# Layer 0's dense mixer takes 512 tokens of two streams in its first products

## The chip, the cores and the metric

The kernel runs on one core of a Trainium2 chip. The metric is the device time of one execution in microseconds (us). Three runs of the kernel before took 2129.68, 2131.46 and 2137.14 us; the median is 2131.46 us.

## The reference, cut to what matters

Two streams of 256 tokens by 1024 features go through two layers with the same weights: the context (CTX) and the latent stream (LAT). Only LAT is returned, so in layer 1 the context is needed for attention keys and values and for the RWKV states alone.

```python
for l in range(DEPTH):                      # DEPTH = 2
    o_lat, o_ctx = token_mixer(modulate(x, ...), modulate(xc, ...), ...)   # attention | RWKV-7 | Hyena
    x  = post_norm(alpha * x + g1 * o_lat, ...)
    xc = post_norm(alpha * xc + cg1 * o_ctx, ...)          # layer 0 only
    if l % 2 == 0:                                         # layer 0: the dense mixer
        f_lat, f_ctx = swiglu(modulate(x, ...), w1, w3, w2), swiglu(modulate(xc, ...), w1, w3, w2)
    else:                                                  # layer 1: experts, LAT only
        f_lat = moe_swiglu(...)
    xc = post_norm(alpha * xc + cg2 * f_ctx, ...)          # layer 0 only
    x  = post_norm(alpha * x + g2 * f_lat, ...)

def swiglu(h, w1, w3, w2):                  # 1024 -> 2816 -> 1024
    return (jax.nn.silu(h @ w1) * (h @ w3)) @ w2
```

In RWKV the latent scan of a layer starts from the final states of that layer's context scan.

## The kernel before, in words

Every weight is fp32 and is used as a pair: `wload` (L348 on) loads a 128x1024 chunk (`raw`, 512 KB by the queue of SP), and `split` (L315, L316) makes `whi` on ACT and the rest `wlo` on DVE. `mm3` (L321 to L323) multiplies two such pairs in three matmuls. Loads are chained in the order of the program (`behind`). The weight buffers have a kind per part of the program (`s.w`, with counts in `BUFS`: raw chunks and split pairs); "l" serves layer 0 and the beginning of layer 1, "n" the rest of layer 1 up to the experts.

The order on each engine is made by the framework's scheduler as the kernel is built: an instruction written earlier has precedence, and one written later may run ahead where the earlier ones wait. `order` adds an edge by hand that one instruction stands behind another. PSUM has eight banks under five tags (`BANKS`): g 3, a 2, w0, w1 and t one each.

The dense mixer (`ffn`) is done for one stream at a time. `hT` normalises and transposes 256 tokens into the pairs `hp`. `block` makes 256 of the 2816 inner features: four weight chunks of `fw13`, each with 8 weight tiles of 128x128 (`ab`, 24 matmuls with 256 columns of tokens), then tanh, gate and split into `ffg`. A stream has 11 blocks in two parts of 6 and 5. After each part `tok_mm` multiplies its `ffg` with `fw2` (`fo`, 512 columns, 12 matmuls a chunk), and `post_norm` gathers the parts (`pnr`), normalises and writes `x`. The last chunks of the last part go through `tok_last`, which finishes the first 128 tokens before the second.

The body (L1688 on) around it: layer 0's output projection for CTX, then Hyena for LAT; the context mixer's `hT`; the output projection for LAT (`wo`, L1290 on); the context mixer, with the modulation products of layer 1 (`ada`, 48 chunks in 3 rounds, fp32) as `fill`: one such chunk after each `wload`; the latent mixer up to its first block of part 2 (`s.some(f, 10)`). Then layer 1: `hT` and seven tiles of the input projection (`win`, `u`) for CTX, `rw_prep` and `rwkv` for CTX, the filter spectra of Hyena (`spectra`), and only then the rest of the latent mixer (`x = s.whole(f)`: four blocks and ten chunks of `fw2`). The latent half of layer 1 follows: `hT`, `win` for RWKV, `rw_prep`, `rwkv`, `win` for attention and the first two Hyena tiles, `attend` (8 rounds), the other Hyena tiles, `hyena`, `w_out`, `moe`.

RWKV has two directions; direction 0 uses bank w0 and direction 1 bank w1 for all its products. `rw_prep` begins with the product `rw` (L855, bank w0). The last step before the chain of states is the multiplication of `rN` (L1075); the chain itself is `rS` (L1089, L1091). `spectra` uses w0 (`hf1`, L542; up to `Kn`, read at L608), w1 and t (`hf_d`, L548).

```python
f = s.ffn(0, LAT, x[LAT])
s.some(f, 10)
s.ldlora(1)
gc = {"st": CTX, "h": s.hT(1, CTX, 0, xc)}
s.win(1, [0, 1, 2, 3, 4, 5, 6], gc)
s.rw_prep(1, gc)
S0 = s.rwkv(1, gc, None, None)
for _ in s.spectra(1, "w0", "t", "w1", *s.spec_load(1)()):
    pass
x = s.whole(f)
```

Of the kernel before, what the change touches and what calls it, by code (L numbers as in the profile page):

```python
# [143 lines left out]
def layout(i):  # L144
# [38 lines left out]
    A["fw13"] = w13(g("ffn_w1"), g("ffn_w3"))[0]  # L183
# [75 lines left out]
class Trunk:  # L259
# [183 lines left out]
    def hT(s, l, st, prm, src, f32=None):  # L443

        nc = s.nc
        dst = s.pairs("hp", "hp", "hp", "hp")
        xh = [s.k([128, 1024], "xhat") for _ in src]
        for i in range(2):
            s.ln_hat(src[i:i + 1], xh[i:i + 1])
        for kp in range(4):  # L450
            ps = s.bank("a", "hT").rearrange("p (k q) -> p k q", k=2)
            for k2 in range(2):
                k = 2 * kp + k2
                for i in range(2):
# [30 lines left out]
    def conv3(s, u, out, cp, cc, cn, bias):  # L485

        nc = s.nc
        if bias is None:
            nc.scalar.activation(out, u, AF.Copy, scale=cc)
        else:  # L490
            nc.scalar.activation(out, u, AF.Identity, scale=cc, bias=bias)
        nc.vector.scalar_tensor_tensor(out[:, 1:], u[:, :255], cp, out[:, 1:], op0=OP.mult, op1=OP.add)
        return nc.vector.scalar_tensor_tensor(out[:, :255], u[:, 1:], cn, out[:, :255], op0=OP.mult, op1=OP.add)


class Mix(Trunk):
# [117 lines left out]
    def hy_in(s, l, g, i, ps):  # L614
# [6 lines left out]
        s.conv3(ps, o, s.pv(l, "hw0", i), s.pv(l, "hw1", i), s.pv(l, "hw2", i), s.pv(l, "hb", i))  # L621
# [133 lines left out]
    def attend(s, l, g, oT):  # L755
# [9 lines left out]
        half, read = [slice(0, 64), slice(64, 128)], None  # L765
# [47 lines left out]
class Rwkv(Mix):  # L813
# [73 lines left out]
    def rw_dir(s, l, g, d, need_y):  # L887
# [258 lines left out]
    def rw_out(s, l, g, oT):  # L1146

        nc = s.nc
        vt, kf, kT = g["vt"], g["kf"], g["kT"]
        pr = s.k([128, 2, 256], "rro")  # L1150
        nc.vector.tensor_add(pr, kf[:, 0], kf[:, 1])
# [30 lines left out]
        nc.scalar.activation(sg[64:96], lo[64:96, :], AF.Tanh, scale=0.5)  # L1182
# [20 lines left out]
class Ffn(Rwkv):  # L1203
# [14 lines left out]
    def post_norm(s, l, st, which, x, parts, apart=()):  # L1218
# [18 lines left out]
        for n, o in enumerate(parts):  # L1237
            for h in range(2):
# [80 lines left out]
    def block(s, b, hp):  # L1319

        nc = s.nc
        ps = [s.bank("g", "ab") for _ in range(2)]
        for kh in range(4):
            hi, lo = s.wload(s.A["fw13"][b, kh])
            for n, p in enumerate(ps):
                for f in range(2):
                    for k in range(2):
                        ws = slice(512 * k + 256 * n + 128 * f, 512 * k + 256 * n + 128 * f + 128)

                        s.mm3(p[:, 256 * f:256 * f + 256], (hi[:, ws], lo[:, ws]), hp[2 * kh + k],  # L1330
                              kh == 0 and k == 0 and f == 0, kh == 3 and k == 1, skip_group_check=True)
# [4 lines left out]
        g = s.k([128, 2, 2, 256], "ffg", F32R)  # L1336
        s.split(t.rearrange("p (f t) -> p f t", f=2), g[:, 0], g[:, 1])
# [18 lines left out]
    def ffn(s, l, st, x):  # L1356

        hp = s.hT(l, st, 3, x)
        yield

        def part(b0, n):
            gt = []

            def o(h):
                for b in range(b0, b0 + n) if h == 0 else ():
                    gt.append(s.block(b, hp))
                    yield
                t2 = lambda i, k: tuple(gt[k // 2][m][:, k % 2, 128 * i:128 * i + 128] for m in range(2))
                banks = [s.bank("g", "fo") for _ in range(2)]
                src = lambda kh: s.A["fw2"][h, b0 + kh]  # L1370
                if h == 1 and b0 > 0:
                    s.tok_mm(src, t2, banks, 2 * n, range(n - 3))
                    s.tok_last([(src(kh), kh, banks) for kh in range(n - 3, n)], t2, 2 * n)
                else:
                    s.tok_mm(src, t2, banks, 2 * n)
# [5 lines left out]
        return (yield from s.post_norm(l, st, 1, x, [part(0, 6), part(6, 5)], (1,)))  # L1381
# [186 lines left out]
class Top(Ffn):  # L1568
# [4 lines left out]
    BUFS = {"a": (12, 0), "l": (6, 4), "n": (5, 4), "m": (30, 4)}  # L1573
# [84 lines left out]
    def body(s):  # L1658
# [64 lines left out]
        x = s.whole(f)  # L1723

        s.w = "n"
# [30 lines left out]
```

## Time and profile before

| what | value |
|---|---|
| median of 3 runs | 2131.46 us |
| the profiled execution's own time | 2134.47 us |
| its span, first to last instruction | 2132.7 us |
| TensorE (PE) busy | 2033.8 us, 95% |
| VectorE (DVE) busy | 1659.7 us, 78% |
| ScalarE (ACT) busy | 1105.6 us, 52% |
| mean granted TensorE clock | 0.965 of full speed |
| HBM read | 464.56 MB |

All times in the views count from the start of the span. Matmuls are pipelined: a matmul's duration overlaps the next one's, so the cost of one in a stream is the distance from start to start. A window's row gives the busy time of each engine with its count of instructions, the granted clock, and the share and rate of the DMA engines. The two layers share the span so: layer 0 up to about 868 us (its mixers up to 516, the dense mixer after that), layer 1 up to the experts from 868 to about 1260, the experts for the rest.

### The profile page before, as it was taken

To read this page: it belongs to the slowest core of one execution; us is meant where nothing else is said; L and a number is where in the kernel's file an instruction comes from. 1 tells how busy PE (TensorE), PEld (TensorE's weight loads), DVE (VectorE), ACT (ScalarE), POOL (GpSimd) and SP (SyncE) were. 2 spreads that over 40 slices of the span, in tenths; PEclk is the share of its full clock that TensorE was granted. 3 is DMA by queue.
4 is the path that set the end of the run, shared out by engine and by line. 5 is a ranking of instruction groups with operands and counts; after the bars stand their busy time and mean duration, and the time that the engine had idled before them with its cause. 6 is when DMAs were issued, how large, how long until landed. Compare 5 with 4: busy or idle time off the path is not lost. (4 is left out here: it accounts for less than half of the span.)

```text
span 2132.7 us, 35433 instructions
## 1 busy us (share of the span) xinstructions
PE 2033.8 (95%) x13514; PEld 1656.6 (78%) x13514; DVE 1659.7 (78%) x3050; ACT 1105.6 (52%) x1615; POOL 111.1 (5%) x87
## 2 busy tenths in 40 slices
PE   7999999999999999989798997999999999999996
PEld 2878777667878999888487676888888888888885
DVE  6897678469753685776888568799899989988997
ACT  3532445132332434443254232877787877778773
POOL 0012002100000000010101200000000000000000
PEclk9999899899999999999998997999999999999998
DMA  8522332246697545332311038699999999999992
GB/s 302 186 83 90 139 124 83 80 160 230 235 337 269 198 164 200 137 102 94 125 55 38 31 110 316 233 329 356 352 347 367 356 343 347 365 359 339 364 352 103
DMA packets 147850, 469.12 MB, mean 220 GB/s; under 512 B 31636, under 2 KB 33972, under 8 KB 147672
## 3 DMA queue, kind: packets, MB, share of 16 engines
q1 hardware_dynamic: 123512, 446.27, 57.9%
q0 software_dynamic: 4816, 17.36, 2.3%
q10 hardware_dynamic: 19344, 3.15, 0.8%
q8 instruction: 108, 1.77, 0.3%
q14 instruction: 70, 0.57, 0.1%
HBM read 464.56 MB, written 2.16 MB: 219 GB/s over the span
## 5 line engine op out<-in xcount | busy, mean ns | idle before, releaser
L316 DVE TENSOR_TENSOR wlo<-wraw,whi 128x1024 fp32r<-128x1024 f32 x748 | 887.4, 1221 | 83.0 <-ACT whi L315 52.4
L315 ACT CAST whi<-wraw 128x1024 fp32r<-128x1024 f32 x748 | 751.6, 1049 | 146.1 <-DMA wraw<-in_fw_dram 33.8
L321 PE MATMUL ab<-whi,m_x 128*128 128x512 f32 x704 | 281.6, 400 | 0.0
L323 PE MATMUL ab<-whi,m_x 128*128 128x512 f32 x704 | 275.6, 391 | 0.0
L322 PE MATMUL ab<-wlo,m_x 128*128 128x512 f32 x704 | 275.0, 391 | 0.0
L321 PE MATMUL ab<-hp,whi 128*128 128x256 f32 x704 | 204.9, 292 | 3.1 <-ACT hp L315 2.2
L323 PE MATMUL ab<-hp,wlo 128*128 128x256 f32 x704 | 201.8, 288 | 2.8 <-DVE wlo L316 2.8
L322 PE MATMUL ab<-hp,whi 128*128 128x256 f32 x704 | 201.4, 286 | 1.3 <-DVE hp L316 1.2
L321 PE MATMUL u<-hp,whi 128*128 128x256 f32 x512 | 152.0, 300 | 3.9 <-ACT hp L315 3.0
L323 PEld LDWEIGHTS ab<-whi,m_x 128*128 128x128 f32 x704 | 132.2, 188 | 28.3
L322 PEld LDWEIGHTS ab<-wlo,m_x 128*128 128x128 f32 x704 | 132.5, 188 | 25.5 <-DVE wlo L316 0.2
L321 PEld LDWEIGHTS ab<-whi,m_x 128*128 128x128 f32 x704 | 132.2, 188 | 25.1
L321 PEld LDWEIGHTS ab<-hp,whi 128*128 128x128 f32 x704 | 135.7, 193 | 19.0 <-issue 10.6
L323 PE MATMUL u<-hp,wlo 128*128 128x256 f32 x512 | 149.0, 294 | 1.4 <-DVE wlo L316 1.1
L322 PE MATMUL u<-hp,whi 128*128 128x256 f32 x512 | 149.5, 295 | 0.0
L323 PEld LDWEIGHTS ab<-hp,wlo 128*128 128x128 f32 x704 | 136.1, 194 | 6.3 <-DVE wlo L316 3.9
L322 PEld LDWEIGHTS ab<-hp,whi 128*128 128x128 f32 x704 | 136.4, 194 | 2.0 <-DVE hp L316 1.8
L321 PE MATMUL mo<-whi,ffg 128*128 128x512 f32 x352 | 137.8, 391 | 0.0
L323 PE MATMUL mo<-whi,ffg 128*128 128x512 f32 x352 | 137.1, 390 | 0.0
L322 PE MATMUL mo<-wlo,ffg 128*128 128x512 f32 x352 | 137.0, 389 | 0.0
L969 POOL TENSOR_TENSOR rBD<-rAT,cst 128x1024 f32<-128x1024 f32 x28 | 67.2, 2408 | 937.7 <-DVE rTm L959 506.9
L321 PEld LDWEIGHTS u<-hp,whi 128*128 128x128 f32 x512 | 99.6, 196 | 18.2 <-issue 9.6
(396 smaller groups left out, 3536.3 us busy)
## 6 DMA issues: line engine op xcount, KB each, us to landing
wraw<-in_mw_dram SPq DMA_DIRECT2D x495, 512.0 KB, 5.6
wraw<-in_fw_dram SPq DMA_DIRECT2D x132, 512.0 KB, 5.7
wraw<-in_adaw_dram SPq DMA_DIRECT2D x96, 512.0 KB, 4.4
wraw<-in_win_dram SPq DMA_DIRECT2D x64, 512.0 KB, 5.1
wraw<-in_mw_dram POOLq DMA_DIRECT2D x33, 512.0 KB, 6.7
wraw<-in_wout_dram SPq DMA_DIRECT2D x24, 512.0 KB, 4.2
lngb<-in_rows_dram SPq DMA_DIRECT2D x12, 512.0 KB, 7.3
x<-in_xs_dram SPq DMA_DIRECT2D x8, 512.0 KB, 5.6
```

Source lines behind the costliest of these rows:

```text
L315: i = (s.nc.scalar.copy if eng == "a" else s.nc.vector.tensor_copy)(hi, src)
L316: return i, s.nc.vector.tensor_sub(lo, src, hi.bitcast(F32))
L321: mm(out, a[0], b[0], start=start, stop=False, **kw)
L322: mm(out, a[0], b[1], start=False, stop=False, **kw)
L323: mm(out, a[1], b[0], start=False, stop=stop, **kw)
L969: i = nc.gpsimd.tensor_mul(x.rearrange("p u (j t) -> p u j t", j=4), bc(ATu[:, :, m, None, :], [128, 8, 4, 32]), bc(mask.rearrange("p (j t ...
```

## The change: what it does

- The dense mixer's blocks take both streams' 512 tokens at once. `fw13` is laid out anew on the host: 22 blocks of 128 features, two chunks each; a chunk's 24 matmuls have 512 columns. A block's two banks come in turn from g and a.
- The blocks go in three parts of 6, 8 and 8. After each of the first two parts the second products (`fw2`) are done for CTX and then LAT; after the third, CTX's are done in `ffn` and LAT's by `x = s.whole(f)`, now right behind layer 1's `hT` for CTX.
- Both streams' `hT` stand before the first block; 15 of the 48 `ada` chunks stand between CTX's and LAT's.
- Layer 1's context half therefore has none of the dense mixer behind it. `s.w = "n"` now holds from CTX's `win` on, with 4 raw chunks and 3 split pairs in place of 5 and 4.
- New edges: in `rw_out` (three uses) the first addition and the tanh of the gate stand behind the last multiplication of `rN` (`fed`); in layer 1's LAT the convolutions of the Hyena tiles and the first product of `attend` stand behind it too.

```diff
-    A["fw13"] = w13(g("ffn_w1"), g("ffn_w3"))[0]
+    u = w13(g("ffn_w1"), g("ffn_w3"))[0].reshape(11, 2, 2, 128, 2, 2, 2, 128)
+    A["fw13"] = np.ascontiguousarray(u.transpose(0, 6, 1, 3, 2, 4, 5, 7)).reshape(22, 2, 128, 4, 256)
...
-    def hT(s, l, st, prm, src, f32=None):
+    def hT(s, l, st, prm, src, dst=None):
-        dst = s.pairs("hp", "hp", "hp", "hp")
+        dst = dst or s.pairs("hp", "hp", "hp", "hp")
...
-    def conv3(s, u, out, cp, cc, cn, bias):
+    def conv3(s, u, out, cp, cc, cn, bias, after=None):
...
+        if after is not None:
+            s.order(i, after)
...
-    def attend(s, l, g, oT):
+    def attend(s, l, g, oT, read=None):
...
+        g["fed"] = fed
...
-        nc.vector.tensor_add(pr, kf[:, 0], kf[:, 1])
+        s.order(nc.vector.tensor_add(pr, kf[:, 0], kf[:, 1]), g["fed"])
...
-        nc.scalar.activation(sg[64:96], lo[64:96, :], AF.Tanh, scale=0.5)
+        s.order(nc.scalar.activation(sg[64:96], lo[64:96, :], AF.Tanh, scale=0.5), fed)
...
     def block(s, b, hp):
-        ps = [s.bank("g", "ab") for _ in range(2)]
-        for kh in range(4):
+        ps = [s.bank("ga"[b % 2], "ab") for _ in range(2)]
+        for kh in range(2):
             hi, lo = s.wload(s.A["fw13"][b, kh])
             for n, p in enumerate(ps):
-                for f in range(2):
-                    for k in range(2):
-                        ws = slice(512 * k + 256 * n + 128 * f, 512 * k + 256 * n + 128 * f + 128)
-                        s.mm3(p[:, 256 * f:256 * f + 256], (hi[:, ws], lo[:, ws]), hp[2 * kh + k],
-                              kh == 0 and k == 0 and f == 0, kh == 3 and k == 1, skip_group_check=True)
+                for k in range(4):
+                    ws = slice(256 * k + 128 * n, 256 * k + 128 * n + 128)
+                    s.mm3(p, (hi[:, ws], lo[:, ws]), hp[4 * kh + k], kh == 0 and k == 0, kh == 1 and k == 3)
...
+    PARTS = (0, 6), (6, 8), (14, 8)
...
+    def ffn(s, l, hp, x):
...
+        out = [s.post_norm(l, st, 1, x[st], [part(st, n) for n in range(3)], (1,), True) for st in range(2)]
+        for n, (b0, nb) in enumerate(s.PARTS):
+            gt[n] = []
+            for b in range(b0, b0 + nb):
+                gt[n].append(s.block(b, hp))
+            if n < 2:
+                for st in range(2):
+                    s.some(out[st], 4)
+        return s.whole(out[CTX]), out[LAT]
...
-    BUFS = {"a": (12, 0), "l": (6, 4), "n": (5, 4), "m": (30, 4)}
+    BUFS = {"a": (12, 0), "l": (6, 4), "n": (4, 3), "m": (30, 4)}
...
-        f = s.ffn(0, CTX, x[CTX])
-        s.some(f, 1)
+        hp, hs = s.ffn_in()
+        s.hT(0, CTX, 3, x[CTX], hs[CTX])
         x.append(s.w_out(0, 1, oT[1], None))
         s.fill = s.ada(1, [0, 1, 2])
-        xc = s.whole(f)
+        s.some(s.fill, 15)
+        s.hT(0, LAT, 3, x[LAT], hs[LAT])
+        xc, f = s.ffn(0, hp, x)
         s.drain()
-        f = s.ffn(0, LAT, x[LAT])
-        s.some(f, 10)
         s.ldlora(1)
         gc = {"st": CTX, "h": s.hT(1, CTX, 0, xc)}
+        x = s.whole(f)
+        s.w = "n"
         s.win(1, [0, 1, 2, 3, 4, 5, 6], gc)
         s.rw_prep(1, gc)
         S0 = s.rwkv(1, gc, None, None)
         for _ in s.spectra(1, "w0", "t", "w1", *s.spec_load(1)()):
             pass
-        x = s.whole(f)
-        s.w = "n"
...
+        gl["hyfed"] = gl["fed"]
         s.win(1, ATT + HY[:2], gl)
-        s.go(s.attend(1, gl, oT))
+        s.go(s.attend(1, gl, oT, gl["fed"]))
```

## Rows read from the trace of the kernel before

**Rows 1.** The page: engines' busy time, and the costliest group of instructions.
```profile
PE 2033.8 (95%) x13514; PEld 1656.6 (78%) x13514; DVE 1659.7 (78%) x3050; ACT 1105.6 (52%) x1615; POOL 111.1 (5%) x87
...
L316 DVE TENSOR_TENSOR wlo<-wraw,whi 128x1024 fp32r<-128x1024 f32 x748 | 887.4, 1221 | 83.0 <-ACT whi L315 52.4
```
**Rows 2.** Windows: stretch, length, busy PE, PEld, DVE, ACT, POOL, clock, DMA.
```profile
516.40:868.00 351.60, 346.73 (x2557) 299.93 (x2557) 219.29 (x354) 130.87 (x158) 0.00 (x0) 0.99 0.65 233
...
868.00:1200.00 332.00, 297.66 (x2605) 251.46 (x2605) 253.98 (x638) 138.69 (x252) 39.41 (x21) 0.95 0.25 80
```
**Rows 3.** Timeline of PE: start, duration, line; ten matmuls lie between the rows.
```profile
800.13 0.28 PE L321 MATMUL ab<-hp,whi 128*128 128x256 f32 x1
...
801.33 0.28 PE L322 MATMUL ab<-hp,whi 128*128 128x256 f32 x1
...
728.07 0.39 PE L322 MATMUL fo<-wlo,ffg 128*128 128x512 f32 x1
...
730.34 0.39 PE L323 MATMUL fo<-whi,ffg 128*128 128x512 f32 x1
```
**Rows 4.** Timeline of PE: one chunk of `ab` between two chunks of `ada`.
```profile
560.86 0.38 PE L321 MATMUL ab<-hp,whi 128*128 128x256 f32 x1
...
563.92 0.64 PE L392 MATMUL ada<-wraw,keep 128*32 128x256 f32 x8
564.49 0.38 PE L321 MATMUL ab<-hp,whi 128*128 128x256 f32 x1
```
**Rows 5.** Start: last `wo` (PE), LAT's second `xhat` (DVE); a window of `wlo` alone.
```profile
516.16 0.40 PE L323 MATMUL wo<-whi,oTh 128*128 128x512 f32 x1
...
555.34 0.81 DVE L441 TENSOR_SCALAR xhat<-x,keep 128x1024 f32<-128x1024 f32 x1
...
516.40:555.40 39.00, 21.27 (x77) 14.52 (x77) 13.32 (x11) 1.00 0.79 266
```
**Rows 6.** Timeline of PE: from CTX's last `fo` to LAT's `ab` at full rate.
```profile
745.98 0.39 PE L323 MATMUL fo<-whi,ffg 128*128 128x512 f32 x1
...
757.82 0.36 PE L321 MATMUL ab<-hp,whi 128*128 128x256 f32 x1
```
**Rows 7.** Timeline of PE: from LAT's last `fo` to layer 1's first `u` of LAT.
```profile
1053.80 0.39 PE L323 MATMUL fo<-whi,ffg 128*128 128x512 f32 x1
...
1066.60 0.69 PE L455 MATMUL hT<-keep,xhat 128*128 128x128 f32 x2 [12.41 <-DVE xhat L441]
...
1070.71 0.58 PE L321 MATMUL u<-hp,whi 128*128 128x256 f32 x1 [0.49 <-ACT hp L315]
```
**Rows 8.** Layer 1: CTX's first `u` and `rS`, LAT's `rw` and last `rN` (durations min/median/max).
```profile
870.55 0.48 PE L321 MATMUL u<-hp,whi 128*128 128x256 f32 x2
...
L1089 PE MATMUL rS<-rS,rMx x56: 218/275/323, 984.3 to 1005.0; 128*128 128x64 f32 x56
...
L855 PE MATMUL rw<-lora,rkl x4: 589/641/693, 1093.9 to 1096.7; 33*128 33x512 f32 x4
...
L1075 DVE TENSOR_TENSOR rN<-rN,keep x4: 680/692/692, 1176.1 to 1199.0; 128x512 f32<-128x512 f32 x4
```
**Rows 9.** Layer 1's spectra: first product on t, first on w0, last reading of w0.
```profile
L548 PE MATMUL hf_d<-hydec,cst x4: 587/640/692, 898.7 to 1006.9; 1*128 1x512 f32 x4
...
L542 PE MATMUL hf<-cst,sn x2: 376/402/427, 995.9 to 996.2; 33*64 33x256 f32 x2
...
1040.47 0.74 DVE L608 SCALAR_TENSOR_TENSOR hyK<-Kn,cst,hy_rb 1x512 f32<-1x512 f32 x1 [0.58 <-PE Kn L606]
```
**Rows 10.** Layer 1's attention: rounds before `rN` is done (x12 is three rounds), two close rounds after.
```profile
1152.00:1199.70 47.70, 4.49 (x12) 1.48 (x12) 1.00 0.04 5
...
1219.41 1.70 PE L774 MATMUL aS<-akv,aq 64*128 64x512 f32 x4
...
1224.85 1.13 PE L774 MATMUL aS<-akv,aq 64*128 64x512 f32 x4
```
**Rows 11.** Windows with `ffs` alone: DVE's work on five blocks' ends, 868 to 1200.
```profile
868.00:1200.00 332.00, 0.00 (x0) 0.00 (x0) 9.68 (x15) 5.46 (x9) 0.95 0.25 80
```

More of the change, by code (lines that the diff above doesn't have):

```diff
@@ L483, in win_steps @@
             yield
-    def conv3(s, u, out, cp, cc, cn, bias):
+    def conv3(s, u, out, cp, cc, cn, bias, after=None):
         nc = s.nc
         if bias is None:
-            nc.scalar.activation(out, u, AF.Copy, scale=cc)
+            i = nc.scalar.activation(out, u, AF.Copy, scale=cc)
         else:
-            nc.scalar.activation(out, u, AF.Identity, scale=cc, bias=bias)
+            i = nc.scalar.activation(out, u, AF.Identity, scale=cc, bias=bias)
+        if after is not None:
+            s.order(i, after)
         nc.vector.scalar_tensor_tensor(out[:, 1:], u[:, :255], cp, out[:, 1:], op0=OP.mult, op1=OP.add)
@@ L620, in hy_in @@
         o = g["hvx"][:, i] if i < 4 else g["hx2z"][:, i - 4]
-        s.conv3(ps, o, s.pv(l, "hw0", i), s.pv(l, "hw1", i), s.pv(l, "hw2", i), s.pv(l, "hb", i))
+        s.conv3(ps, o, s.pv(l, "hw0", i), s.pv(l, "hw1", i), s.pv(l, "hw2", i), s.pv(l, "hb", i),
+                g.get("hyfed"))
         if i in (1, 3):
@@ L764, in attend @@
         vals = s.akv[l][:, 1, :ns].rearrange("p a b -> p (a b)")
-        half, read = [slice(0, 64), slice(64, 128)], None
+        half = [slice(0, 64), slice(64, 128)]
         for i in range(4):
@@ L1148, in rw_out @@
         nc = s.nc
-        vt, kf, kT = g["vt"], g["kf"], g["kT"]
+        vt, kf, kT, fed = g["vt"], g["kf"], g["kT"], g["fed"]
         pr = s.k([128, 2, 256], "rro")
-        nc.vector.tensor_add(pr, kf[:, 0], kf[:, 1])
+        s.order(nc.vector.tensor_add(pr, kf[:, 0], kf[:, 1]), g["fed"])
         nc.vector.tensor_mul(pr, pr, kT)
@@ L1216, in rows_late, with post_norm @@
             return s.rows(l, i)
-    def post_norm(s, l, st, which, x, parts, apart=()):
+    def post_norm(s, l, st, which, x, parts, apart=(), pause=False):
         nc = s.nc
@@ L1248, in post_norm @@
                     read(n, h, i, src)
+                if pause:
+                    yield
         y = s.two("x")
@@ L1335, in block @@
         nc.vector.scalar_tensor_tensor(t, t, 0.5, ps[1], op0=OP.mult, op1=OP.mult)
-        g = s.k([128, 2, 2, 256], "ffg", F32R)
-        s.split(t.rearrange("p (f t) -> p f t", f=2), g[:, 0], g[:, 1])
+        g = s.k([128, 2, 512], "ffg", F32R)
+        s.split(t, g[:, 0], g[:, 1])
         return g[:, 0], g[:, 1]
@@ L1354, in gated, with ffn_in, part @@
         gt.append((g[:, 0], g[:, 1]))
[L1356 to L1362, printed above, removed]
-            def o(h):
[L1365 to L1373, printed above, removed]
+    PARTS = (0, 6), (6, 8), (14, 8)
+    def ffn_in(s):
+        t = [s.k([128, 2, 512], "hp", F32R) for _ in range(8)]
+        cut = lambda st: [(h[:, 0, 256 * st:256 * st + 256], h[:, 1, 256 * st:256 * st + 256]) for h in t]
+        return [(h[:, 0], h[:, 1]) for h in t], [cut(CTX), cut(LAT)]
+    def ffn(s, l, hp, x):
+        gt = {}
+        def part(st, n):
+            b0, nb = s.PARTS[n]
+            def o(h):
+                cs = lambda i: slice(256 * st + 128 * i, 256 * st + 128 * i + 128)
+                t2 = lambda i, k: tuple(q[:, cs(i)] for q in gt[n][k])
+                banks = [s.bank("ga"[h] if n < 2 else "g", "fo") for _ in range(2)]
+                src = lambda kh: s.A["fw2"][h, b0 // 2 + kh]
+                nc = nb // 2
+                if h == 1 and n == 2:
+                    s.tok_mm(src, t2, banks, nb, range(nc - 3))
+                    s.tok_last([(src(kh), kh, banks) for kh in range(nc - 3, nc)], t2, nb)
                 else:
-                    s.tok_mm(src, t2, banks, 2 * n)
+                    s.tok_mm(src, t2, banks, nb)
                 yield
@@ L1379, in part @@
             return o
-        return (yield from s.post_norm(l, st, 1, x, [part(0, 6), part(6, 5)], (1,)))
+        out = [s.post_norm(l, st, 1, x[st], [part(st, n) for n in range(3)], (1,), True) for st in range(2)]
[7 more added lines that the diff above has]
+        return s.whole(out[CTX]), out[LAT]
     def moe_route(s, l, x, acc):
```

## The prediction

> **What bounds the kernel now.** I read the page first: PE is busy 95% of the span, DVE 78%, and the costliest group is DVE's weight split, 1.221 us a chunk [rows 1]. Then the windows: in the dense mixer (516 to 868) PE is busy nearly all the time, with DMA at 0.65 and DVE at 219 of 352 us; in layer 1 up to LAT's `rN` (868 to 1200) DVE is busy 254.0 of 332 us and PE seems full only because the dense mixer's rest fills it [rows 2]. So two limits have to be priced apart: a stream of matmuls in the first stretch, a chain of waits in the second.
>
> The timeline gives the price of a matmul in a stream: ten with 256 columns start within 1.20 us, ten with 512 within 2.27 us, so 0.120 and 0.227 us [rows 3]. A chunk with one `ada` chunk behind it takes 564.49 - 560.86 = 3.63 us; less 24 x 0.120 that is 0.75 us for the `ada` chunk [rows 4]. With these the stretch to 868 can be rebuilt: 18 blocks x 96 x 0.120 = 207.4, 34 `fw2` chunks x 12 x 0.227 = 92.6, 48 `ada` chunks x 0.75 = 36, together 336 of 352; the other 16 us are waits, most of them when LAT's tokens are not ready [rows 6].
>
> The second limit is read from what waits for what in layer 1. The spectra's first product on bank t runs at 898.7, but their first on w0 only at 995.9, while CTX's `rS` chain is ending (984.3 to 1005.0) [rows 8, 9]. Ready work of the spectra thus stood almost 100 us behind the RWKV that owns w0 and w1: these two single banks are handed out in the order of the program. LAT's `rw` also needs w0. So CTX's RWKV, the spectra and LAT's RWKV stand in line, whatever else is free.
>
> **The change part by part.** I sum by landmarks, from the last `wo` at 516.2 to the end of LAT's last `rN`, 1199.0 + 0.7 = 1199.7 [rows 5, 8]; what follows is kept apart.
>
> *First products.* 2112 matmuls x 0.120 = 253.4 us become 1056 x 0.227 = 239.7: 13.7 us less. The granted clock is 0.99 there, the upper level, so the price is that of full speed. The split and the load of 44 chunks go too (44 x 1.221 = 53.7 us of DVE, 23 MB), but DVE and DMA are not the limit in this stretch [rows 1, 2]: nothing. The page "TensorE: Matmul & The Clock Gate" of the Trainium skill, section "Back-to-back issue gap", speaks against this step: it gives N/2.4 ns and 2.5 more, 109.2 ns and 215.8, by which joining pairs would save only 1056 x 2.6 ns = 2.7 us. The rows show a fixed part of 2 x 120 - 227 = 13 ns, not 2.5; the measurement decides.
>
> *Second products.* 528 matmuls x 0.227 = 119.9 us in both kernels. All of them, and all blocks, now lie ahead of layer 1; before, four blocks (46.1 us) and ten chunks (27.2 us) lay in its holes. This is the change's main charge: 73 us of PE work leaves a place where it was partly free.
>
> *The start.* Both streams' `hT` now come before the first block. LAT's second `xhat` is done 39.2 us after the last `wo`; in that time DVE also made 13.3 us of weight splits and two blocks' ends, 2 x 1.9 us, of the 9.7 us that five take [rows 5, 11]. Without these it is 22 us, and from there the first product follows after 4.1 us, as at LAT's later `hT` [rows 7], with two splits (2.4 us) ahead: 28 us. It can't be under 21 us, and not over 39. The 15 `ada` chunks (11 us of PE) lie inside this wait; on SP's queue they are 7.9 MB ahead of the first `fw13` chunk, 30 us at the 266 GB/s of that stretch [rows 5], but the first six raw buffers fill while `wo` runs, so the load is not later than the tokens. The wait of 11.8 us at LAT's later start [rows 6] is gone.
>
> *The rest.* 33 `ada` chunks x 0.75 = 24.8. For switches of work I take 3. CTX's end (16.9 us from its last `fo` to its first `u`, by [rows 7]) is covered by LAT's third part, 96 x 0.227 = 21.8 us; uncovered it would be 17. CTX's first `u` is then at 516.2 + 28 + 239.7 + 119.9 + 24.8 + 3 = 931.6, against 870.6 [rows 8]: 61 us later.
>
> *The chain in layer 1.* Before, from the first `u` to the end of CTX's `rS`: 1005.3 - 870.6 = 134.7; from there to the last reading of w0: 1041.2 - 1005.3 = 35.9; LAT's `rw` then came only at 1093.9, 52.7 us later, since LAT's blocks, its 16.9 us end and its `win` stood between; from `rw` to the last `rN`: 105.8 [rows 7 to 9]. After, LAT's tokens and `win` are done while w0 is busy, so the 52.7 us go. The three pieces also lose neighbours. Of the 26 chunks of the dense mixer, 16 x 1.221 = 19.5 us of DVE go from the first, but LAT's norm, `hT` and `win` take their place there: between 115 (all gained) and 143 (the newcomers cost eight more); I take 128. The spectra lose six splits, 7.3 us, half of them in their way: 28.6 to 35.9; I take 32. LAT's piece had eight `win` tiles beside it (9.8 us of splits) which will mostly be done before: 86 to 106; I take 94. Sum 254. LAT's last `rN` ends at 931.6 + 254 = 1185.6: 14.1 us earlier.
>
> *The tail and the edges.* Three of eight attention rounds ran before `rN` was done; now none may. Two close rounds lie 5.4 us apart [rows 10], so 0 to 16 us; most fits where attention waited for RWKV's last products, and I take 4. The edges in `rw_out` move two early instructions behind `rN` in two layers; their engines have holes on both sides: nothing, and 1 to 2 us each if they have none. "n" with 4 and 3 buffers: a tile takes PE 2.9 us and one split 1.2, so two pairs suffice; nothing. SP's queue gets layer 1's loads earlier, in the same order.
>
> Net: -14.1 + 4 = -10.1 us. The profiled execution's own time is 2134.47 (span 2132.7 and 1.8 around it), 3.0 over the median of the three runs; 2134.5 - 10.1 = 2124.4 on its scale, 2121.4 on the median's.
>
> **The rivals.** *Slower: the line of w0 keeps its length.* If the newcomers slow CTX's RWKV, the spectra and LAT's piece as much as the dense mixer did, the three pieces stay 276.4, and `rN` ends at 1208.0; with the tail +12.3, so 2143.8. It decides from a sum of 264 on. For it: LAT's norm and `win` are heavy on DVE, and DVE is busy 254 of 332 us already. Against: each piece loses work of the dense mixer. Chance 0.22.
>
> *Much faster: DVE is the only bound.* DVE's 254.0 less 31.7 (26 splits) and 9.7 [rows 2, 11] is 212.6 us, under the 229.6 of the three lower bounds. With these `rN` ends at 1161.2; without the tail's charge that is -38.5: 2093. For it: DVE's holes came from a PE queue full of the dense mixer. Against: RWKV's own steps wait for each other in any case. Chance 0.20.
>
> *No change: the start.* If LAT's tokens take the whole 39 us, the first `u` comes 11 us later and the net is +1: 2132. For it: DVE is busy with CTX's `hT` when LAT's norm begins. Against: the splits that stood between are lower in precedence now. Chance 0.15. *No change: the pair is no cheaper.* If 512 columns with tokens moving cost twice 256, less 2.6 ns, by the stated rule, 11 us are missing: 2132.5. Against: `fo` has the same shape, with other operands. Chance 0.05.
>
> **How the numbers follow.** The forecast case (gain of 4 to 20 us, 2111 to 2128 by itself) holds 0.38. A measurement of this kernel tells about 0.3%, 6.4 us, from no change. Faster by more: 0.36 of the forecast and 0.20, 0.56. Within: 0.02 and the two cases of no change, less 0.02 that end slower, 0.20. Slower: 0.22 and 0.02, 0.24. The range goes from the fast rival, 2093, to just beyond the slow one, 2146.
>
> **What would show it.** Right: `ab` at 0.227 us start to start; LAT's `rw` directly behind the last reading of w0; first `u` of CTX near 932; no wait like those at 746 and 1054. Wrong: `rw` of LAT on w0 before the spectra end (then the line is no line and the gain is larger), CTX's `u` after 945, or more than 10 us added behind `rN`.

## The result, and the profile after

The changed kernel takes **2188.95 us** (median of 4 runs, 2185.73 to 2196.93), against 2132.14 us for the kernel before on the same chip: ratio 1.0269, 95% interval 1.0233 to 1.0305, so 57 us slower. The forecast was 2121.4 us, range 2093 to 2146: wrong in sign, and outside the range. The two profiled executions lie 2189.8 - 2132.7 = 57.1 us apart.

First the engines' totals and the costliest group on the page of the changed kernel (beside [rows 1]).

```profile
PE 2043.4 (93%) x12458; PEld 1615.0 (74%) x12458; DVE 1619.9 (74%) x3022; ACT 1070.6 (49%) x1571; POOL 108.8 (5%) x87
...
L318 DVE TENSOR_TENSOR wlo<-wraw,whi 128x1024 fp32r<-128x1024 f32 x704 | 845.6, 1223 | 116.8 <-ACT whi L317 88.4
```

The change did what it says: 13514 - 12458 = 1056 matmuls and 44 weight splits fewer. The time rose all the same, so more work is not the cause. Where it went is read by landmarks. Below are PE's last `wo` of layer 0 and its first `ab`, then the start and end of layer 1's chain up to LAT's last `rN`, all from the timeline (start, duration, engine, line; in brackets the idle time before and what ended it).

```profile
542.72 0.39 PE L325 MATMUL wo<-whi,oTh 128*128 128x512 f32 x1
...
569.17 1.08 PE L323 MATMUL ab<-hp,whi 128*128 128x512 f32 x2
...
958.94 0.61 PE L457 MATMUL hT<-keep,xhat 128*128 128x128 f32 x2 [2.49 <-DVE xhat L443]
964.78 1.54 PE L457 MATMUL hT<-keep,xhat 128*128 128x128 f32 x6 [5.23 <-DVE xhat L443]
967.01 0.58 PE L323 MATMUL u<-hp,whi 128*128 128x256 f32 x1 [0.68 <-ACT hp L317]
...
1112.36 0.48 DVE L1096 SCALAR_TENSOR_TENSOR rS<-rS,keep,rN 128x64 f32<-128x64 f32 x2 [0.18 <-PE rS L1094]
...
1137.68 1.90 PE L610 MATMUL Kn<-hy_eo,cst 128*32 128x512 f32 x4
1139.52 0.61 PE L716 MATMUL ass<-cst,mx 128*128 128x2 f32 x4
1140.05 1.98 PE L860 MATMUL rw<-lora,rkl 33*128 33x512 f32 x4
...
1246.84 0.69 DVE L1080 TENSOR_TENSOR rN<-rN,keep 128x512 f32<-128x512 f32 x1 [8.88 <-PE rN L1078]
```

Against the same landmarks of before [rows 5, 7 to 9], in us of one profile each. All are starts (the "end" of `rS` is DVE's last `rS`, that of `rN` its last `rN`); before, the very first `u` starts at 869.97 and the last `rS` on DVE at about 1005.5. The last `wo` of layer 1 starts at 1303.6 before and 1357.4 after:

| stretch | before | after | forecast |
|---|---|---|---|
| start to last `wo` of layer 0 | 516.2 | 542.7 | 516.2 |
| last `wo` to first `u` of CTX | 353.8 | 424.3 | 415.4 |
| first `u` to end of CTX's `rS` | 135.5 | 145.6 | 128 |
| end of `rS` to LAT's `rw` | 88.4 | 27.5 | 32 |
| LAT's `rw` to last `rN` | 105.1 | 106.7 | 94 |
| last `rN` to last `wo` of layer 1 | 104.6 | 110.6 | 108.6 |
| from there to the end | 829.1 | 832.4 | 829.1 |

The row that is furthest above the forecast, by 26.5 us, lies in layer 0, **ahead of the code that the change is named after**: there it put nothing but two scheduling edges in `rw_out`. The stretch from last `wo` to last `wo` takes 814.7 instead of 787.4, 27.3 more; the rest 3.3. Together 57.1.

Windows of the changed kernel (stretch, length, busy PE, PEld, DVE, ACT, POOL, clock, DMA): start wait, mixer, layer 1 to the end of `rN`, and one stretch of it.

```profile
542.70:570.40 27.70, 13.22 (x151) 8.00 (x150) 26.91 (x85) 5.85 (x11) 0.00 (x0) 0.69 0.55 207
570.40:956.40 386.00, 385.71 (x1849) 300.16 (x1847) 191.09 (x264) 114.22 (x137) 0.00 (x0) 1.00 0.50 171
...
967.00:1247.50 280.50, 238.84 (x2162) 198.03 (x2162) 194.21 (x546) 104.04 (x207) 38.64 (x22) 0.86 0.14 40
...
1175.00:1200.00 25.00, 9.44 (x42) 9.07 (x42) 19.98 (x109) 6.87 (x16) 4.18 (x2) 0.55 0.12 23
```

In the mixer PE is full at a clock of 1.00 while DVE is busy half the time (191 of 386 us); in layer 1 PE has holes and the mean granted clock is 0.86 (0.95 before [rows 2]), in the last stretch, with PE busy 9.4 of 25 us, 0.55. Before, the mixer's rest lay in layer 1. How much of the longer pieces is this lower clock, no run separates.

### The profile page after: what moved, and what is told of

It is laid out like the page before. It is cut to its first block, busy times and chain, and to the rows that moved or that the text cites. A ratio compares the mean times of both kernels' runs of the same rounds, so it can differ in the third digit from the quotient of the medians.

```text
span 2189.8 us, 33022 instructions
## 1 busy us (share of the span) xinstructions
PE 2043.4 (93%) x12458; PEld 1615.0 (74%) x12458; DVE 1619.9 (74%) x3022; ACT 1070.6 (49%) x1571; POOL 108.8 (5%) x87
## 5 line engine op out<-in xcount | busy, mean ns | idle before, releaser
L318 DVE TENSOR_TENSOR wlo<-wraw,whi 128x1024 fp32r<-128x1024 f32 x704 | 845.6, 1223 | 116.8 <-ACT whi L317 88.4
L317 ACT CAST whi<-wraw 128x1024 fp32r<-128x1024 f32 x704 | 721.5, 1050 | 316.4 <-PE ab L325 92.1
L323 PE MATMUL u<-hp,whi 128*128 128x256 f32 x512 | 154.1, 303 | 3.5 <-ACT hp L317 2.3
L324 PE MATMUL u<-hp,whi 128*128 128x256 f32 x512 | 151.8, 298 | 4.1 <-DVE hp L318 4.1
L323 PE MATMUL ab<-hp,whi 128*128 128x512 f32 x352 | 139.8, 398 | 0.0
L324 PE MATMUL ab<-hp,whi 128*128 128x512 f32 x352 | 137.1, 390 | 0.0
L325 PE MATMUL ab<-hp,wlo 128*128 128x512 f32 x352 | 137.0, 390 | 0.0
L323 PEld LDWEIGHTS u<-hp,whi 128*128 128x128 f32 x512 | 101.3, 199 | 15.6 <-issue 7.5
L325 PEld LDWEIGHTS u<-hp,wlo 128*128 128x128 f32 x512 | 101.3, 198 | 15.4 <-DVE wlo L318 11.3
L324 PEld LDWEIGHTS u<-hp,whi 128*128 128x128 f32 x512 | 101.5, 199 | 8.9 <-DVE hp L318 4.4
L1339 DVE SCALAR_TENSOR_TENSOR ffs<-ffs,ab 128x512 f32<-128x512 f32 x22 | 15.1, 688 | 104.1 <-ACT ffs L1338 104.1
```

Source lines behind the costliest of these rows:

```text
L317: i = (s.nc.scalar.copy if eng == "a" else s.nc.vector.tensor_copy)(hi, src)
L318: return i, s.nc.vector.tensor_sub(lo, src, hi.bitcast(F32))
L323: mm(out, a[0], b[0], start=start, stop=False, **kw)
L324: mm(out, a[0], b[1], start=False, stop=False, **kw)
L325: mm(out, a[1], b[0], start=False, stop=stop, **kw)
L1339: nc.vector.scalar_tensor_tensor(t, t, 1.0, ps[0], op0=OP.add, op1=OP.mult)
```

## The experiments

Three theories. **A, the edges**: the two edges in `rw_out` change the order of layer 0's RWKV. **B**: layer 0 is slower by the mixer's move, buffers or tokens. **C, the cover**: the rest of the loss is that LAT's third part, its norm, `hT` and `win` now stand beside CTX's end and RWKV. Ratios are against the kernel before on the same chip. "wo to wo" is the stretch from the last `wo` of layer 0 to that of layer 1 in the run's own profile (787.4 before, 814.7 changed).

**The edges alone, and all but the edges.** The first kernel is the one before with these two lines; the second is the changed one without them.

```diff
-        nc.vector.tensor_add(pr, kf[:, 0], kf[:, 1])
+        s.order(nc.vector.tensor_add(pr, kf[:, 0], kf[:, 1]), g["fed"])
...
-        nc.scalar.activation(sg[64:96], lo[64:96, :], AF.Tanh, scale=0.5)
+        s.order(nc.scalar.activation(sg[64:96], lo[64:96, :], AF.Tanh, scale=0.5), fed)
```

> The kernel before with nothing of the change but the two edges in rw_out (the add of kf and the tanh of the gate both placed behind the last instruction that feeds the RWKV products). Theory A (the two edges change the order in which layer 0's RWKV pieces are issued, and that costs layer 0 about 26 us and layer 1 up to 13 us more): last wo of layer 0 at about 543 us instead of 516, time 2155 to 2172. Theory B (the lost time of layer 0 comes from the mixer's move, its buffers or its tokens): last wo at 516 to 518, time 2130 to 2136.

> The changed kernel without the two edges in rw_out. Theory A: last wo of layer 0 at 516 us instead of 542.7, layer 1 the same or some 10 us shorter, time 2150 to 2163. Theory B: last wo at 540 or later, time 2183 to 2193. Theory C (what is left against the kernel before comes from layer 1, where the dense mixer no longer covers CTX's end and LAT's norm and win share DVE with CTX's RWKV): time 2150 to 2163 too, with 25 us or more between first u and the end of rN than the 254 us of the forecast.

Measured: 2165.75 us, ratio 1.0150 (1.0109 to 1.0191), and 2165.61 us, ratio 1.0162 (1.0132 to 1.0192). The two last `wo`, each from its timeline:

```profile
543.03 0.48 PE L323 MATMUL wo<-whi,oTh 128*128 128x512 f32 x1
```
```profile
517.57 0.40 PE L325 MATMUL wo<-whi,oTh 128*128 128x512 f32 x1
```

Theory A holds and B falls, if 543 is not one execution's luck (see the repeat below): with nothing of the mixer changed the edges move the `wo` to 543.0; without them the changed kernel has it at 517.6. By medians they cost 32 us (23 to 41) on the kernel before. From wo to wo this kernel takes 790.8, so next to nothing of it is in layer 1. How it begins, the timelines of DVE and ACT show. Kernel before, CTX's RWKV of layer 0:

```profile
113.41 0.68 DVE L1151 TENSOR_TENSOR rro<-rkf 128x512 f32<-128x512 f32 x1
...
135.87 1.12 ACTq L1016 DMA_DIRECT2D rD<-rTm  x2
...
142.79 0.28 DVE L1014 TENSOR_REDUCE rTm<-rTm 128x8 f32<-128x128 f32 x1
143.10 1.10 ACTq L1016 DMA_DIRECT2D rD<-rTm  x2
...
144.46 1.22 DVE L1020 TENSOR_TENSOR rTT<-keep,cst 128x1024 f32<-128x1024 f32 x1
...
151.68 1.23 DVE L1020 TENSOR_TENSOR rTT<-keep,cst 128x1024 f32<-128x1024 f32 x1
```

The same with the two edges alone:

```profile
133.81 1.12 ACTq L1016 DMA_DIRECT2D rD<-rTm  x2
...
142.58 1.21 DVE L1020 TENSOR_TENSOR rTT<-keep,cst 128x1024 f32<-128x1024 f32 x1
...
145.17 0.28 DVE L1014 TENSOR_REDUCE rTm<-rTm 128x8 f32<-128x128 f32 x1
145.48 1.10 ACTq L1016 DMA_DIRECT2D rD<-rTm  x2
...
151.95 0.69 DVE L1037 TENSOR_TENSOR rKA<-rKA,rPQ 128x512 f32<-128x512 f32 x1 [0.25 <-PE rPQ L1031]
154.32 0.69 DVE L1037 TENSOR_TENSOR rKA<-rKA,rPQ 128x512 f32<-128x512 f32 x1 [1.68 <-PE rPQ L1031]
156.32 0.16 DVE L713 COPY keep<-ass 128x4 f32<-128x4 f32 x1 [1.31 <-PE ass L711]
...
158.11 1.22 DVE L1020 TENSOR_TENSOR rTT<-keep,cst 128x1024 f32<-128x1024 f32 x1
...
208.09 2.27 DVE L1152 TENSOR_TENSOR rro<-rkf 128x512 f32<-128x512 f32 x1
```

The add of `kf` was early (113.4) and is now after `rN` (208.1); that itself costs nothing. But hyena's steps stand in its place, and the order of what follows is another. RWKV's two directions run their triangular solve (`rTm`) side by side; ACT sends each result off (`rD`) to become an `rTT`. Before, the second `rTT` came 7.2 us after the first, now 15.5. Of these, 11.7 us already lie between the ends of the two solves (133.81 and 145.48; 7.2 before). The rest is DVE's order: the second `rTT` stands behind the first direction's two `rKA` steps and attention's `ass`, all of which wait for PE. In the changed kernel the gap is 165.2 - 149.1 = 16.1 us.

CTX's part of this loss is nearly made good again: LAT's `rw` in layer 0 starts at 251.6 us against 250.7. What lasts comes from LAT's RWKV. Its last multiplications of `rN`, kernel before and the edges alone:

```profile
L1075 DVE TENSOR_TENSOR rN<-rN,keep x4: 679/692/692, 376.8 to 395.9; 128x512 f32<-128x512 f32 x4
```
```profile
L1075 DVE TENSOR_TENSOR rN<-rN,keep x4: 691/692/692, 383.7 to 426.8; 128x512 f32<-128x512 f32 x4
```

There too one direction lags (the two `rTT` start 8.4 us apart instead of 1.2), and the last `rN` starts 30.9 us later; of that 26.9 is left at the last `wo`. In the changed kernel that `rN` starts at 425.4. The edges reach the order through what they displace.

**Which of them.** The edges in layer 1 alone (`if l == 1` around both), and the tanh's edge alone. The add's edge alone was not tried.

> The changed kernel with the two edges in rw_out in layer 1 alone. Theory A with all its cost in layer 0: last wo at 516 us and time 2160 to 2164 (26 us less), LAT's rw to the end of rN as in the changed kernel, 107 us. Theory A with a cost in layer 1 too: this kernel is slower than the one without the edges by 8 to 13 us, all of it between LAT's rw and the end of rN. Theory B: 2183 to 2193.

> The changed kernel with the edge of the gate's tanh kept and the edge of the add of kf taken out. Theory A by the add (the add keeps a vector tile and DVE's order): last wo at 516 us, time 2150 to 2163. Theory A by the tanh (ScalarE's order): last wo at 540 us or more, time 2180 to 2192. Theory B: 2183 to 2193 whichever edge stays.

Measured: 2155.26 us, 1.0115 (1.0078 to 1.0152), last `wo` at 517.6, `rw` to the end of `rN` 108.4; and 2171.70 us, 1.0199 (1.0164 to 1.0235), last `wo` at 523.1. So the cost is in layer 0; in layer 1 the edges charge nothing that these runs can tell. With the tanh's edge alone the second solve is late only in LAT's RWKV (`rTT` at 342.1 and 356.3, 14 us apart; last `rN` at 410.2). Its time is under that with both edges and can't be told from that without: the intervals overlap, and 523.1 lies among the profiles without edges (see the end). So the tanh's edge alone is not the whole cause. Whether the add's edge alone is, or it takes both, stays open.

**The place of LAT's third part, and the banks of the spectra.** All four without the two edges in `rw_out`; the first edit gives the spectra other banks, the second moves LAT's rest behind them, the third does both, and the fourth takes only the edge off layer 1's attention (`s.attend(1, gl, oT)`).

```diff
-        for _ in s.spectra(1, "w0", "t", "w1", *s.spec_load(1)()):
+        for _ in s.spectra(1, "a", "a", "t", *s.spec_load(1)()):
...
-        x = s.whole(f)
         s.w = "n"
...
+        x = s.whole(f)
         gl = {"st": LAT, "h": s.hT(1, LAT, 0, x)}
```

> The changed kernel without the two edges in rw_out, and with layer 1's spectra on the banks a, a and t instead of w0, t and w1. Line theory (LAT's rw waits only because w0 and w1 are handed out in the order of the program): LAT's rw no longer comes after the spectra's last Kn but directly behind CTX's last rS, at about 1083 us instead of 1109.7, and the end of rN comes up to 26 us earlier, near 1203 to 1215; time 2140 to 2155. Rival (LAT's rw is late for another reason: its tokens, its win tiles or DVE's load): rw at 1105 or later, time 2160 to 2172. Second rival (the line is real, but DVE's work only moves): rw near 1083 and the end of rN within 6 us of 1229, time 2158 to 2168.

> The changed kernel without the two edges in rw_out, and with LAT's third part and its post_norm placed behind layer 1's spectra in the order of the program, where the kernel before had its own rest of the dense mixer. Cover theory (LAT's norm, hT and win take DVE from CTX's end and from CTX's RWKV): from CTX's last fo to the first u 17 to 20 us instead of 24 or more, from the first u to the end of rS 128 to 133 us instead of 139.7, LAT's rw still directly behind the last Kn, time 2145 to 2156. Rival (CTX's RWKV has its own length, whatever stands beside it): 136 to 141 us from the first u to the end of rS; the time moves by the earlier start alone, 2155 to 2163. Second rival (LAT comes too late and its rw waits for tokens): rw over 10 us after the last Kn, time 2165 or more.

> Both edits together: layer 1's spectra on banks a, a and t, and LAT's third part behind them, without the two edges in rw_out. If the line and the cover are both costs of their own, the gains add: 2120 to 2140. If freeing the line only helps while LAT's tokens are there early, this gives no more than the late third part alone.

> The changed kernel without the two edges in rw_out and without the edge that holds layer 1's attention behind RWKV's last feeding instruction. Forecast's term (the edge charges about 4 us at the tail): first aS round before the end of rN, end of the last wo 2 to 8 us earlier than 1332, time 2157 to 2164. Rival (rounds that come early take DVE and ScalarE from the rN chain, so that nothing is gained): the end of rN later than 1229 by what the tail gains, time 2162 to 2170.

Measured, with the stretches of the table above (us):

| kernel | ratio (95%) | `wo` to `u` | to `rS` end | to `rw` | to `rN` end | to `wo` | wo to wo |
|---|---|---|---|---|---|---|---|
| no edges | 1.0162 (1.0132-1.0192) | 425.2 | 139.7 | 27.2 | 119.3 | 103.2 | 814.6 |
| spectra's banks | 1.0043 (1.0013-1.0072) | 425.4 | 150.0 | 3.1 | 110.1 | 106.1 | 794.7 |
| late LAT | 1.0048 (1.0018-1.0078) | 408.3 | 127.6 | 43.3 | 109.7 | 101.9 | 790.8 |
| both | 1.0091 (1.0059-1.0123) | 408.5 | 148.6 | 36.0 | 114.1 | 103.5 | 810.7 |
| free attention | 1.0122 (1.0058-1.0185) | 424.8 | 139.4 | 27.2 | 106.1 | 111.1 | 808.6 |

The place of LAT's part costs what Theory C says, in size: the late part alone gives 24 us by ratios and by wo to wo. Its timeline:

```profile
903.08 0.69 PE L457 MATMUL hT<-keep,xhat 128*128 128x128 f32 x2 [12.41 <-DVE xhat L443]
907.14 0.58 PE L323 MATMUL u<-hp,whi 128*128 128x256 f32 x1 [0.43 <-ACT hp L317]
...
1067.41 1.90 PE L610 MATMUL Kn<-hy_eo,cst 128*32 128x512 f32 x4
...
1077.95 1.12 PE L860 MATMUL rw<-lora,rkl 33*128 33x512 f32 x2
```

PE now stands idle 12.41 us at CTX's end, just as at LAT's end before [rows 7], and yet the first `u` is 17 us earlier after the `wo`. In the changed kernel the 21.8 us of LAT's products fill that hole, and DVE has LAT's norm (`pnt`, `pnr`) among CTX's own steps: two waits for `xhat`, 2.49 and 5.23 us. 21.8 - 12.4 + 2.5 + 5.2 = 17. Of this, 9.4 us is work that must be done somewhere in any case; the 7.7 us of waits is what the cover itself charges up to the first `u`. CTX's RWKV takes 127.6 us, as in the forecast, with 211 `u` matmuls in that stretch instead of 419. LAT's `rw` is 9 us later than the last `Kn`, not directly behind it as this run's forecast had it: until then PE is busy with LAT's `win`.

The banks prove the line of w0: with others, `rw` follows `rS` by 3.1 us instead of 27.2, and 20 us are gained. But the spectra then run beside CTX's RWKV, which takes 150.0 (148.6 with the late part too); together the two edits take longer than either alone (810.7 from wo to wo against 794.7 and 790.8), which neither forecast had. Freeing attention gave 6 us in one profile and an interval that overlaps that of no edges.

**Other places, same idea.** Late part and no edge on attention; spectra behind LAT's `rwkv` on banks a, a, t, with and without that edge; LAT's third part between CTX's `rwkv` and the spectra.

> LAT's third part behind the spectra, as before, and besides no edge that holds layer 1's attention (so of the new edges only the one on hyena's convolution stays). By the two single runs, from the last wo of layer 0 to the last wo of layer 1: 790.8 us with the late part, 6 us less for the free attention: 785, against 787.4 in the kernel before and 814.7 in the changed one; time 2130 to 2142. If attention's early rounds only help while LAT's win is done early, there is no gain: 790 and 2138 to 2146.

> LAT's third part behind CTX's RWKV, and the spectra on banks a, a and t behind LAT's RWKV in the order of the program, without the two edges in rw_out. Line theory with the cover kept: 128 us from CTX's first u to the end of rS as with the late part alone, then LAT's rw as soon as its tokens and win are there, 15 to 30 us after rS, 110 to 118 us to the end of rN; from last wo to last wo 765 to 782, time 2110 to 2135. Rival (the spectra's DVE work, some 30 us, must lie somewhere and each place lengthens the chain beside it): from last wo to last wo 788 to 800, time 2138 to 2155.

> As the one with the spectra behind LAT's RWKV, and without the edge on attention. If the edge charges the tail 6 us whatever stands before it: 4 to 8 us less than with the edge. If attention then competes with the spectra for banks a and t: the same or up to 10 us more.

> LAT's third part and post_norm between CTX's RWKV and the spectra in the order of the program; nothing else but the two edges in rw_out taken out. If what matters is that LAT's part stands behind CTX's end and RWKV: 128 us from first u to the end of rS, rw behind the last Kn without the 9 us that it was late, from last wo to last wo 780 to 788, time 2128 to 2142. If LAT's tail between RWKV and spectra delays the spectra on w0: last Kn over 36 us behind rS, 790 to 800.

Measured: ratios 1.0067 (1.0039 to 1.0096), 1.0006 (0.9979 to 1.0034), 1.0028 (1.0000 to 1.0056), 1.0002 (0.9966 to 1.0039); wo to wo 799.4, 794.0, 796.5, 790.1. With the spectra behind LAT's RWKV, `rw` comes 11.2 us after `rS` and `rN` ends 249 us after the first `u` instead of 281, as the line theory says; but the tail takes 136.8 us instead of some 104. The spectra now stand ahead of attention's own steps on DVE (its last `mx<-rope` starts 28 us after the end of `rN`, at 1203.3; with the late part alone 41 us before it, at 1147.3), and of the tail 30 us ran at a granted clock of 0.50, the lower of its two levels; how much of the longer tail is that, no run separates:

```profile
1190.00:1220.00 30.00, 30.00 (x191) 23.81 (x189) 14.62 (x65) 5.26 (x9) 0.00 (x0) 0.50 0.00 1
```

Of these four the free attention brought no gain (799.4), and the spectra's place was a miss (794.0, in the rival's bounds). None falls under 790. The 128 us forecast for CTX's RWKV were missed too: 133 and 135 with the spectra behind LAT's RWKV, and 139.6 with LAT's part between RWKV and the spectra, where `rw` came 30.0 us after `rS` instead of 43.3. So a shorter CTX's RWKV is not by itself a gain: the same 790 come out with 127.6 and with 139.6.

**What stays open, and the wait.** The kernel before once more, for a second profile; and LAT's third part as in the last kernel above, with the first 4 or 6 of 22 blocks made for each stream alone (`block_st`: `block` with one stream's 256 columns, each chunk loaded and split once per stream), CTX's in the place of the 15 `ada` chunks; with 6 also LAT's `hT` placed first. The edit with six:

```diff
-        s.some(s.fill, 15)
+        done = [s.k([128, 2, 512], "ffg", F32R) for _ in range(6)]
+        for b, g in enumerate(done):
+            s.block_st(b, hs[CTX], CTX, g)
         s.hT(0, LAT, 3, x[LAT], hs[LAT])
-        xc, f = s.ffn(0, hp, x)
+        for b, g in enumerate(done):
+            s.block_st(b, hs[LAT], LAT, g)
+        xc, f = s.ffn(0, hp, x, [(g[:, 0], g[:, 1]) for g in done])
```

> The kernel before once more, for a second profile of it. Theory A (layer 0 loses its time by the order that the two edges in rw_out make): last wo of layer 0 between 498 and 527 us, as in the six profiles without both edges. Rival (its 516 was one of the lucky executions, and layer 0 spreads up to 543 with one and the same order): 530 or later.

> LAT's third part behind CTX's RWKV, no edges in rw_out, and the first four of the 22 first-product blocks made for each stream alone with 256 columns, CTX's ahead of LAT's hT in the order of the program, in place of the 15 ada chunks. Wait theory (with both streams in one product, nothing can start until LAT's tokens are there: 26.7 us in every such kernel, which is the main part of what the joint products can't win back): CTX's four blocks, 4 x 48 x 0.120 = 23 us, lie inside the wait; from the last wo to the first ab 2 to 6 us, from last wo to first u 408.4 less 12 to 20; from last wo to last wo 770 to 780, time 2115 to 2130. Rival (the splits of these blocks delay LAT's hT on DVE by as much): first u at 404 us or more after the last wo, time 2132 to 2142.

> As the one with four blocks, with six (35 us of CTX's products). Wait theory: 3 to 8 us less than with four, since 39 us pass until LAT's tokens are there; each block that is made apart costs 2 x 48 x 0.120 - 48 x 0.227 = 0.6 us. Rival: the same or slower than with four, by two blocks' splits on DVE.

> As the one with six blocks, but LAT's hT ahead of CTX's six blocks in the order of the program. If DVE's order decides the wait (hT before the splits): LAT's tokens 5 to 15 us earlier, PE with holes in the first 20 us; the time within 6 us of the one with the blocks first. If the order of the program does not decide: the same within 2 us from last wo to last wo.

Measured: the kernel before again 2135.23 us, 1.0002 (0.9975 to 1.0029), last `wo` at 511.9. With four blocks 2131.57 us, 0.9997 (0.9971 to 1.0022), wo to wo 788.5; with six **2123.02 us, 0.9968 (0.9939 to 0.9997)**, wo to wo 778.5; with `hT` first 2138.97 us, 1.0015 (0.9989 to 1.0041), 786.1. The start with six, from PE's timeline:

```profile
515.88 0.40 PE L325 MATMUL wo<-whi,oTh 128*128 128x512 f32 x1
517.91 0.39 PE L323 MATMUL ab<-hp,whi 128*128 128x256 f32 x1
...
915.83 0.69 PE L457 MATMUL hT<-keep,xhat 128*128 128x128 f32 x2 [12.41 <-DVE xhat L443]
919.88 0.58 PE L323 MATMUL u<-hp,whi 128*128 128x256 f32 x1 [0.43 <-ACT hp L317]
```

The wait is gone (2.0 us instead of 26.7), but the first `u` is only 4.4 us earlier (404.0 against 408.4), with four blocks not at all (408.6): the forecasts of 770 to 780 and of 12 to 20 us were misses for four, and six came to the edge. Of the 24.7 us that the wait lost, the 15 `ada` chunks that lay in it took 11 back and the six blocks' own products 6 x 0.6 = 4: they now lie in the full stretch. That would leave 10 us with six blocks and 11 with four, where 4.4 and -0.2 were measured. The forecast's 0.6 us a block leaves out that a block made apart is split twice: with six, 12 x 1.22 = 15 us more of DVE, which is busy 39.5 of the first 40 us after the `wo`. That this is the rest was not tested. With `hT` first the forecast (within 6 us of the other) was a miss: 16 us more by medians.

The version with six blocks has the lowest median of all: under the kernel before by 0.03 to 0.61%, under the changed one by 3%. As the best of many tries, so near to no change and with no repeat of its own, its gain on the kernel before is not certain.

**Do the two costs add?** The changed kernel with both edges and the late part; and six blocks apart without the edge on attention.

> The changed kernel with nothing altered but the place of LAT's third part and post_norm: behind layer 1's spectra; both edges in rw_out stay. If the two costs are each on their own, layer 0 ends near 543 us, the stretch from last wo to last wo takes 786 to 800 us instead of 814.7, and the time is 24 us under the changed kernel's and 23 to 34 over the same kernel without the edges: 2160 to 2172. If the edges cost nothing once layer 1 is covered: 2138 to 2150. If the place costs nothing with the edges: 2184 or more.

> The kernel with six blocks made apart, and without the edge that holds layer 1's attention behind RWKV. If that edge charges the tail as in the pair measured without the apart blocks (6 us by single runs): 2112 to 2122, from the end of rN to the last wo 4 to 8 us less, or the end of rN earlier. If the early rounds take as much from rN's chain as they give the tail, as with the late third part: 2122 to 2134.

Measured: 2180.82 us, 1.0218 (1.0178 to 1.0257), last `wo` at 546.9, wo to wo 800.5; and 2132.12 us, 1.0013 (0.9984 to 1.0041), wo to wo 786.7. The edges charge layer 0 for the third time; the time of this kernel, 2180.8, lies between the forecasts, above 2160 to 2172 and under 2184. The edge on attention is no charge: without it the time is not shorter, here as with the late part. The four combinations, in per cent over the kernel before: edges and early part 2.69, early alone 1.62, edges and late part 2.18, late alone 0.48. So the edges cost 1.07 (23 us) or 1.70 (36 us), the early part 0.51 or 1.14 (11 or 24 us), together 2.21 of 2.69 (47 of 57 us). Whether they simply add is open: the difference, 0.63, is no larger than the four intervals taken together (some 0.7). What is left, 0.48 (10 us, 4 to 17), is the price of all the rest of the change: the joint products with their wait and their three parts, the smaller buffers, the edges on hyena and attention. Of these only the wait and the edge on attention were varied.

## Why the prediction was wrong, and where it was right

**Wrong: "nothing, and 1 to 2 us each if they have none".** The edges in `rw_out` were priced by the two instructions that they hold back. They cost 26.5 us in layer 0 of the profile and 23 to 36 us by medians, the largest single term of the miss. Their engines do have holes. What was overlooked is that an edge is an input to the whole order: hyena's steps took the free places, one of RWKV's two directions fell behind the other, and in LAT's RWKV the last `rN` came 30 us later. No rival of the prediction was in layer 0 at all.

**Wrong: "covered by LAT's third part".** The 21.8 us of products do lie in the hole; but the third part brings its norm on DVE, and the first `u` came 424.3 us after the `wo`, not 415.4. From PE's last `fo` (956.1) to the first `u` (967.0) there are 10.9 us where the sum had none. With the part late and the hole open it is 408.3; by the prediction's own terms, 415.4 - 21.8 + 16.9 = 410.5.

**Wrong: "between 115 and 143; I take 128"** (measured 145.6, above the upper end, in the changed kernel) and **"I take 94"** (106.7, just over its upper end of 106). The newcomers of the first piece were underrated: 419 `u` matmuls lie in it instead of 168. It is 127.6, 128.3 and 129.0 in the three profiles with LAT behind the spectra on w0, 138 to 146 in those with LAT's norm, `hT` and `win` beside it, 148.6 and 150.0 with the spectra beside it. (Two profiles of the kernel before gave 135.5 and 139.6, so differences under 5 us say nothing.) DVE's load alone does not set its length: DVE is busy 107 us in it in the changed kernel and also with LAT late, where it takes 127.6. Whether it is the order on DVE, the granted clock (0.86 against 0.94) or the smaller weight buffers ("n" with 4 and 3, priced at nothing and never varied) stays open.

The second had the wrong reason: the `win` tiles did go, and the piece got no shorter. `u` in it, before and after (first PE, then PEld):

```profile
1093.90:1199.70 105.80, 30.95 (x193) 25.83 (x192) 2.86 (x6) 5.62 (x14) 0.94 0.12 32
```
```profile
1140.05:1247.50 107.45, 4.76 (x24) 4.08 (x24) 0.00 (x0) 2.55 (x6) 0.83 0.07 16
```

Without the tiles PE waits for DVE, for a step of attention (`mx`) and for RWKV's own solve:

```profile
1181.16 1.12 PE L998 MATMUL rtr<-keep,rkdb 128*128 128x128 f32 x4 [7.51 <-DVE mx L700]
...
1201.40 0.98 PE L1036 MATMUL rPQ<-rKA,rTT 128*128 128x128 f32 x3 [10.81 <-DVE rTT L1025]
```

The slow rival, "the line of w0 keeps its length" (2143.8), had this part right: the three pieces, 145.6 + 27.5 + 106.7 = 279.8 against its 276.4. The fast one falls: DVE was busy 194 of 280.5 us, so it was not the only bound.

**Right.** What the change is named after came as forecast. The start: forecast 28 us, measured 542.7 to 569.2, 26.5, and 26.7 without the edges. The mixer: 239.7 + 119.9 + 24.8 + 3 = 387.4 forecast, 386.0 measured. The pitch: ten intervals below, 2.28 us, so 0.228 each, and the rival "the pair is no cheaper" falls.

```profile
602.20 0.39 PE L324 MATMUL ab<-hp,whi 128*128 128x512 f32 x1
...
604.48 0.39 PE L325 MATMUL ab<-hp,wlo 128*128 128x512 f32 x1
```

LAT's `rw` directly behind the last reading of w0: 1140.05, after `Kn`'s products; forecast 32 us from `rS`, measured 27.5. The rows give 2 x 120 - 228 = 12 ns gained a pair. The rule that the prediction sets against this, from the page "TensorE: Matmul & The Clock Gate" of the Trainium skill, section "Back-to-back issue gap", is given there for an isolated matmul, not for a stream of weight loads and matmuls like this one.

Luck: the tail. 4 us were forecast for the edge on attention and 6.0 measured, but without this edge no time was gained, and in the profiles that have it, with the spectra ahead of LAT's RWKV, this stretch spreads from 102 to 123.

Sum of the misses in the one profile, by the rows of the table: 26.5 (layer 0), 424.3 - 415.4 = 8.9, 145.6 - 128 = 17.6, 27.5 - 32 = -4.5, 106.7 - 94 = 12.7, 110.6 - 108.6 = 2.0, 832.4 - 829.1 = 3.3: 66.5 us, from the forecast of -10 to 57. Layer 0 is 26.5 of it, the four stretches from there to the last `rN` together 34.7.

## What to carry to other kernels

Price a scheduling edge by the order that it makes, not by the instruction that it holds: look at which ready work will take the free place and which wait then stands ahead of the critical chain, in every use of the function that has the edge. Work that fills a hole of one engine brings its own work for another; moved work is cheap only where both have room. Here 12.4 us of idle PE were filled, and 7.7 us of new waits for DVE came of it. And a piece of a chain that loses its neighbours need not get shorter: look first whether it waited for them or for itself.

## What the hardware showed that was not expected

Layer 0 ends at very different times with the same work. In 16 profiles with neither edge in layer 0 the last `wo` starts between 498.1 and 526.8 us, the kernel before among them at 516.2 and 511.9. Windows from the start to that `wo`, of the latest (spectra's banks) and the earliest (late and banks):

```profile
0.00:526.80 526.80, 502.11 (x4020) 377.48 (x4020) 375.51 (x1023) 192.94 (x381) 49.97 (x32) 0.95 0.42 142
```
```profile
0.00:498.10 498.10, 474.77 (x4019) 361.26 (x4020) 374.40 (x1023) 192.81 (x381) 50.06 (x32) 0.99 0.44 150
```

The counts and DVE's busy time agree; PE's busy time and the granted clock (0.95 and 0.99) do not. Why the clock differs stays open. In 400 to 450 us the mean granted clock was 0.73 in one profile (no edges) and 1.00 in another (late LAT). A single profile of this kernel can thus be 28 us off in one layer: the stretch from `wo` to `wo` and the medians had to be read beside each other, and the 6 us of the free attention, from single profiles, did not hold.
